# RMSNorm with GELU on one core: two rows a partition, gamma by matmul, VectorE in program order

## The chip, the cores and the metric

One core of one Trainium2 chip. The time is the device time of one execution in microseconds; the median of several runs is quoted. "Span" is the profiled execution, which is 1.8 us shorter than the time of the same run (333.7 against 335.53 before).

## The reference

```python
batch, seq_len, hidden = 8, 1024, 2048          # float32
rms = np.sqrt(np.mean(x ** 2, axis=-1, keepdims=True) + eps)
out = gamma * x / rms
return (0.5 * out * (1 + np.tanh(np.sqrt(2 / np.pi) * (out + 0.044715 * out ** 3)))).astype(np.float32)
```

There are 8192 rows of 2048 numbers. 67.1 MB are read and 67.1 MB written, and nothing is reused but gamma.

## The kernel before

A tile is 128 rows, one row a partition, 1 MB. Tiles are handled in groups of 4, then 2, then 1. Per tile: a load, a multiply by gamma on VectorE (into bf16), a square with a sum on ScalarE or VectorE (its elementwise result goes to PSUM, the accumulator memory, and is thrown away). Per group: eleven small VectorE steps that compute 1/rms. Then per tile a GELU on ScalarE, which writes over the tile's x buffer, and a store.

```python
    # group_sizes: 4 while more than 8 tiles are left, 2 while more than 4, then 1
    x_pool = ctx.enter_context(tc.tile_pool(name="xbuf", bufs=12))
    g_pool = ctx.enter_context(tc.tile_pool(name="gbuf", bufs=8))
    psum_pool = ctx.enter_context(tc.tile_pool(name="psum", bufs=2, space=bass.MemoryType.PSUM))

    gamma_sb = singles.tile([P, D], fp32)
    nc.sync.dma_start(out=gamma_sb, in_=gamma.partition_broadcast(P))
    # ... cut ...
    def emit_post(prev):
        tiles_p, xbufs_p, gbufs_p, inv_rms_p = prev
        for j, ti in enumerate(tiles_p):
            nc.scalar.activation(out=xbufs_p[j], in_=gbufs_p[j],
                func=mybir.ActivationFunctionType.Gelu_apprx_tanh, scale=inv_rms_p[:, j : j + 1])
            nc.scalar.dma_start(out=out_flat[ti * P : (ti + 1) * P, :], in_=xbufs_p[j])

    for ig, gsz in enumerate(group_sizes):
        # ... cut ...
        n_scalar_sq = gsz // 2
        for j, ti in enumerate(tiles):
            bx = x_pool.tile([P, D], fp32, name="bx")
            nc.sync.dma_start(out=bx, in_=x_flat[ti * P : (ti + 1) * P, :])
            bg = g_pool.tile([P, D], bf16, name="bg")
            nc.vector.tensor_tensor(out=bg, in0=bx, in1=gamma_sb, op=mybir.AluOpType.mult)
            scratch = psum_pool.tile([P, D], fp32, name="sq_scratch")
            if j < n_scalar_sq:
                nc.scalar.activation(out=scratch, in_=bx, ..., accum_out=ssq[:, j : j + 1])   # square
            else:
                nc.vector.tensor_tensor_reduce(out=scratch, in0=bx, in1=bx, ..., accum_out=ssq[:, j : j + 1])
        # ... cut: eleven steps of VectorE, ssq -> u -> yb -> w -> inv_rms, for the whole group ...
        if prev is not None:
            emit_post(prev)
        prev = (tiles, xbufs, gbufs, inv_rms)
    emit_post(prev)
```

The order of instructions in the text is not the order on the engines: the framework's scheduler sets that before the program is built, as the timeline in the prediction shows.

## Time and profile before

| | before |
|---|---|
| median of 4 runs | 335.43 us (335.31 to 335.54) |
| profile span | 333.7 us |
| VectorE, ScalarE busy | 249.0, 185.8 us |
| moved by the transfer engines | 135.32 MB in 18582 packets, mean 405 GB/s |
| VectorE waiting for loads of x | 67.1 us in 41 waits |

The page cuts the span into 40 equal slices and gives for each the busy tenths of every engine and the GB/s that the transfer engines moved. A packet is one piece of a transfer as the profile records it. The lines themselves are in the prediction below.

### The profile page before, as it was taken

To read this page: it belongs to the slowest core of one execution; us is meant where nothing else is said; L and a number is where in the kernel's file an instruction comes from. 1 tells how busy PE (TensorE), PEld (TensorE's weight loads), DVE (VectorE), ACT (ScalarE), POOL (GpSimd) and SP (SyncE) were. 2 spreads that over 40 slices of the span, in tenths; PEclk is the share of its full clock that TensorE was granted. 3 is DMA by queue.
4 is the path that set the end of the run, shared out by engine and by line. 5 is a ranking of instruction groups with operands and counts; after the bars stand their busy time and mean duration, and the time that the engine had idled before them with its cause. 6 is when DMAs were issued, how large, how long until landed. Compare 5 with 4: busy or idle time off the path is not lost.

```text
span 333.7 us, 850 instructions
## 1 busy us (share of the span) xinstructions
DVE 249.0 (75%) x353; ACT 185.8 (56%) x126; POOL 0.2 (0%) x4
## 2 busy tenths in 40 slices
DVE  0999998397785959768587876959777695956950
ACT  1442996748548274764728467373945824460391
POOL 0000000000000000000000000000000000000000
DMA  7999399999999999999999999999999999999298
GB/s 310 424 424 424 160 380 422 425 428 428 429 426 425 427 431 427 426 426 429 429 424 425 427 430 428 426 425 428 429 427 425 426 430 428 425 425 428 104 408 346
DMA packets 18582, 135.32 MB, mean 405 GB/s; under 512 B 2064, under 2 KB 2064, under 8 KB 2064
## 3 DMA queue, kind: packets, MB, share of 16 engines
q1 hardware_dynamic: 9360, 68.16, 48.4%
q10 hardware_dynamic: 9216, 67.11, 48.0%
q14 instruction: 6, 0.05, 0.0%
HBM read 68.16 MB, written 67.11 MB: 405 GB/s over the span
## 4 chain that ended last, share of the span: by engine, by line
DMA 80%; DVE 12%; ACT 4%; issue 1%; SPq 0%; ACTq 0%; DVEq 0%
DMA out_dram<-bx 74%; DMA bx<-in_x_dram 6%; DVE sq_scratch L107 6%; DVE bg L92 5%; ACT bx L62 4%; ACTq L68 0%; SPq L88 0%; DVE u L119 0%; DVE yb L133 0%; DVE w L141 0%; DVE w L140 0%; DVE yb L126 0%; DVE ssq L107 0%; DVE inv_rms L152 0%; DVE w L144 0%
## 5 line engine op out<-in xcount | busy, mean ns | idle before, releaser
L92 DVE TENSOR_TENSOR bg<-bx,gamma_sb 128x2048 bf16<-128x2048 f32 x64 | 146.3, 2290 | 67.2 <-DMA bx<-in_x_dram 67.1
L62 ACT ACTIVATE bx<-bg,inv_rms 128x2048 f32<-128x2048 bf16 x64 | 124.6, 1994 | 44.2 <-DVE inv_rms L169 23.1
L99 ACT ACTIVATE sq_scratch<-bx 128x2048 f32<-128x2048 f32 x30 | 56.2, 1874 | 96.2 <-DMA out_dram<-bx 50.9
L107 DVE CUSTOM_DVE_ANT_0 sq_scratch<-bx 128x2048 f32<-128x2048 f32 x34 | 77.4, 2307 | 0.0
L99 ACT ACTIVATION_READ_ACCUMULATOR sq_scratch<-bx 128x1 f32 x30 | 5.6, 186 | 0.0
L107 DVE DVE_READ_ACCUMULATOR2_ANT ssq<- 128x1 f32 x34 | 4.8, 142 | 0.0
L161 DVE TENSOR_SCALAR w<-w 128x4 f32<-128x4 f32 (+2 forms) x20 | 3.2, 166 | 0.5
L144 DVE TENSOR_SCALAR w<-w 128x4 f32<-128x4 f32 (+2 forms) x20 | 3.2, 166 | 0.4
L158 DVE TENSOR_TENSOR w<-w,u 128x4 f32<-128x4 f32 (+2 forms) x20 | 3.1, 161 | 0.5
L155 DVE TENSOR_TENSOR w<-inv_rms 128x4 f32<-128x4 f32 (+2 forms) x20 | 3.1, 160 | 0.5
L169 DVE TENSOR_TENSOR inv_rms<-inv_rms,w 128x4 f32<-128x4 f32 (+2 forms) x20 | 3.1, 160 | 0.5
L152 DVE TENSOR_TENSOR inv_rms<-yb,w 128x4 f32<-128x4 f32 (+2 forms) x20 | 3.1, 160 | 0.5
L141 DVE TENSOR_TENSOR w<-w,u 128x4 f32<-128x4 f32 (+2 forms) x20 | 3.1, 160 | 0.4
L133 DVE TENSOR_TENSOR yb<-magic_sb,yb 128x4 int32<-128x4 int32 (+2 forms) x20 | 3.1, 160 | 0.4
L140 DVE TENSOR_TENSOR w<-yb 128x4 f32<-128x4 f32 (+2 forms) x20 | 3.1, 160 | 0.4
L119 DVE TENSOR_SCALAR u<-ssq 128x4 f32<-128x4 f32 (+2 forms) x20 | 3.2, 162 | 0.2
L126 DVE TENSOR_SCALAR yb<-u 128x4 int32<-128x4 int32 (+2 forms) x20 | 3.1, 161 | 0.1
L99 ACT ACT_TABLE_LOAD x1 | 1.3, 1283 | 0.7 <-PEq L197 0.7
L62 ACT ACT_TABLE_LOAD x1 | 1.3, 1283 | 0.0
L57 DVE MEMSET magic_sb<- 128x4 int32 x1 | 0.1, 62 | 0.8 <-PEq L197 0.8
L197 POOL MEMSET const-bfloat16-1.0<- 128x1 bf16 x1 | 0.1, 101 | 0.0
L197 POOL MEMSET const-uint8-127<- 128x1 uint8 x1 | 0.1, 101 | 0.0
(2 smaller groups left out, 0.2 us busy)
## 6 DMA issues: line engine op xcount, KB each, us to landing
bx<-in_x_dram SPq DMA_DIRECT2D x64, 1024.0 KB, 10.4
out_dram<-bx ACTq DMA_DIRECT2D x64, 1024.0 KB, 19.5
gamma_sb<-in_gamma_dram SPq DMA_DIRECT2D x1, 1024.0 KB, 4.8
```

The source lines that it names most:

```text
L62: nc.scalar.activation(out=xbufs_p[j], in_=gbufs_p[j], func=mybir.ActivationFunctionType.Gelu_apprx_tanh, scale=inv_rms_p[:, j : j + 1],)
L92: nc.vector.tensor_tensor(out=bg, in0=bx, in1=gamma_sb, op=mybir.AluOpType.mult)
L99: nc.scalar.activation(out=scratch, in_=bx, func=mybir.ActivationFunctionType.Square, scale=inv_sqrt_d, accum_out=ssq[:, j : j + 1],)
L107: nc.vector.tensor_tensor_reduce(out=scratch, in0=bx, in1=bx, scale=1.0 / D, scalar=0.0, op0=mybir.AluOpType.mult, op1=mybir.AluOpType.add ...
L119: nc.vector.tensor_scalar(out=u[:, g], in0=ssq[:, g], scalar1=float(eps), scalar2=None, op0=mybir.AluOpType.add,)
L126: nc.vector.tensor_scalar(out=yb[:, g], in0=u[:, g].bitcast(i32), scalar1=1, scalar2=None, op0=mybir.AluOpType.logical_shift_right,)
L133: nc.vector.tensor_tensor(out=yb[:, g], in0=magic_sb[:, g], in1=yb[:, g], op=mybir.AluOpType.subtract,)
L140: nc.vector.tensor_tensor(out=w[:, g], in0=y0, in1=y0, op=mybir.AluOpType.mult)
L141: nc.vector.tensor_tensor(out=w[:, g], in0=w[:, g], in1=u[:, g], op=mybir.AluOpType.mult)
L144: nc.vector.tensor_scalar(out=w[:, g], in0=w[:, g], scalar1=-0.5, scalar2=1.5, op0=mybir.AluOpType.mult, op1=mybir.AluOpType.add,)
L152: nc.vector.tensor_tensor(out=inv_rms[:, g], in0=y0, in1=w[:, g], op=mybir.AluOpType.mult)
L161: nc.vector.tensor_scalar(out=w[:, g], in0=w[:, g], scalar1=-0.5, scalar2=1.5, op0=mybir.AluOpType.mult, op1=mybir.AluOpType.add,)
```

## The change

The intent: two consecutive rows a partition, so that a load or a store is 2 MB and each partition's piece is 16 KB in one run; 8 x buffers of 2 MB in place of 12 of 1 MB; groups of one chunk at the head and at the tail, of two in the middle; of each chunk, one row's square on ScalarE and the other's on VectorE; gamma read as one 8 KB row and spread to the partitions by a matmul with ones instead of a 1 MB broadcast; and VectorE's instructions kept in the order of the program. The core of the diff (cut: the same renaming in the loop, and the eleven steps, which don't change):

```diff
+R = 2
+NXBUF = 8
+NGBUF = 4
...
+        x_wide = x_flat.rearrange("(a r) d -> a (r d)", r=R)
+        out_wide = out_flat.rearrange("(a r) d -> a (r d)", r=R)
...
+        head = [1, 1]
+        tail = [1, 1, 1, 1]
+        mid_size = 2
...
-    x_pool = ctx.enter_context(tc.tile_pool(name="xbuf", bufs=12))
-    g_pool = ctx.enter_context(tc.tile_pool(name="gbuf", bufs=8))
+    x_pool = ctx.enter_context(tc.tile_pool(name="xbuf", bufs=NXBUF))
+    g_pool = ctx.enter_context(tc.tile_pool(name="gbuf", bufs=NGBUF))
...
-    nc.sync.dma_start(out=gamma_sb, in_=gamma.partition_broadcast(P))
+    gamma_row = singles.tile([1, D], fp32)
+    nc.scalar.dma_start(out=gamma_row, in_=gamma.rearrange("(o d) -> o d", o=1))
+    ones_row = singles.tile([1, P], fp32)
+    nc.vector.memset(ones_row, 1.0)
+    gamma_ps = psum_pool.tile([P, D], fp32, name="sq_scratch")
+    for k in range(D // 512):
+        nc.tensor.matmul(
+            gamma_ps[:, k * 512 : (k + 1) * 512],
+            lhsT=ones_row,
+            rhs=gamma_row[:, k * 512 : (k + 1) * 512],
+            start=True,
+            stop=True,
+        )
+    nc.vector.tensor_copy(out=gamma_sb, in_=gamma_ps)
...
-            if j < n_scalar_sq:
+                    on_scalar = r == 0
...
-        tile_rmsnorm_gelu_kernel(tc, *args)
+        with tc.manual_schedule(engines={_mybir.EngineType.DVE}):
+            tile_rmsnorm_gelu_kernel(tc, *args)
```

## The prediction

> **What bounds the kernel now.** I read the page first: the engines' shares, then the 40 slices, then the chain that ended last.
>
> ```profile
> DVE 249.0 (75%) x353; ACT 185.8 (56%) x126; POOL 0.2 (0%) x4
> DMA  7999399999999999999999999999999999999298
> GB/s 310 424 424 424 160 380 422 425 428 428 429 426 425 427 431 427 426 426 429 429 424 425 427 430 428 426 425 428 429 427 425 426 430 428 425 425 428 104 408 346
> DMA packets 18582, 135.32 MB, mean 405 GB/s; under 512 B 2064, under 2 KB 2064, under 8 KB 2064
> DMA 80%; DVE 12%; ACT 4%; issue 1%; SPq 0%; ACTq 0%; DVEq 0%
> ```
>
> No compute engine is full (VectorE 75%), but the transfers are at 9 tenths in 36 of the 40 slices, at one flat rate of about 427 GB/s. The chain is 80% transfers. So the kernel is bound by bytes over 427 GB/s, except in four slices that stand out: 0 (310), 4 (160), 37 (104) and 39 (346). I cut the span there with the table by stretches (columns: length, VectorE, ScalarE, GpSimd busy, granted clock, DMA share, GB/s).
>
> ```profile
> 2.00:34.00 32.00, 25.60 (x20) 10.96 (x12) 0.00 (x0) 1.00 1.01 421
> 34.00:39.00 5.00, 4.82 (x20) 4.68 (x5) 0.00 (x0) 1.00 0.08 33
> 39.00:57.00 18.00, 16.45 (x21) 13.84 (x8) 0.00 (x0) 1.00 0.98 388
> 57.00:311.00 254.00, 191.71 (x235) 143.41 (x98) 0.00 (x0) 1.00 1.01 427
> 311.00:317.00 6.00, 6.00 (x38) 2.47 (x2) 0.00 (x0) 1.00 0.03 11
> 317.00:333.00 16.00, 4.39 (x24) 9.21 (x5) 0.00 (x0) 1.00 0.95 393
> ```
>
> There are two holes. The reads of gamma and of the first 12 tiles (all the x buffers there are) end near 34 us; no store is in flight until 39, because ScalarE's first GELU starts at 36.67. Near the end, the stores that were queued run out at 311 and the next begins at 317. The timeline tells why in both places: VectorE isn't late for want of speed, its order is bad.
>
> ```profile
> 24.02 0.16 DVE L119 TENSOR_SCALAR u<-ssq 128x4 f32<-128x4 f32 x1
> 24.10 2.28 DVE L92 TENSOR_TENSOR bg<-bx,gamma_sb 128x2048 bf16<-128x2048 f32 x1
> 26.30 0.16 DVE L126 TENSOR_SCALAR yb<-u 128x4 int32<-128x4 int32 x1
> 26.37 2.29 DVE L92 TENSOR_TENSOR bg<-bx,gamma_sb 128x2048 bf16<-128x2048 f32 x1
> 28.57 0.15 DVE L133 TENSOR_TENSOR yb<-magic_sb,yb 128x4 int32<-128x4 int32 x1
> ...
> 314.53 3.89 ACT L62 ACTIVATE bx<-bg,inv_rms 128x2048 f32<-128x2048 bf16 x2 [14.68 <-DVE inv_rms L169]
> ```
>
> The first group's sum of squares is complete at 24.0, and its eleven small steps (0.2 us apart where nothing comes between) would end near 26.2. They are interleaved with the next group's 2.29 us passes and end at 36.6. At the end ScalarE waits 14.68 us for the same kind of result.
>
> **What the Trainium skill says.** "DMA: Bandwidth & Descriptors", section Specifications, gives a fabric ceiling of 435 GB/s for a core; the trace agrees, 427 in the middle. The same page, section "Issuing engines are not separate DMA queues", says that queues of different engines interleave on the same 16 engines; the trace agrees: the two queues hold 48.4% and 48.0%, and reads alone (421 from 2 to 34 us, its ramp included) are no faster than reads and writes together. "VectorE: DVE Perf Modes", section "Why PSUM operands drop a tier", says that a float32 operand in PSUM leaves VectorE at its basic rate; no copy from PSUM is in this trace, so I take the 2.29 us of a 128x2048 pass for it. So the big passes and the transfer rate are both near what they can be, and what is left to win is bytes and holes.
>
> **The change, part by part.**
>
> *Gamma.* The 1.05 MB broadcast goes; an 8 KB row takes its place. At 427 GB/s that takes 2.5 us off the transfers. Added: four matmuls and one VectorE copy. The first multiply began at 8.10. Now: row landed at about 3 us (a guess, from the 2.2 us after which the first bytes came before), some 4 to 6 us for four cold float32 matmuls (a guess, no matmul is in this trace), 2.3 for the copy: 9 to 11 us. A late start of up to 3 us, off the path unless it opens the first hole again.
>
> *VectorE in program order.* Per 2 MB chunk (two rows a partition): two multiplies and one square, 2.2 us apart each and 0.14 for the read, 6.8 us; then 2.2 us for the small steps per group. The first group is one chunk: 10.5 + 6.8 + 2.2 = 19.5 us, GELU twice 1.99, so the first store is issued near 24 us instead of 40.6 (the second row's end is what issues it).
>
> *More x buffers.* 8 x 2 MB instead of 12 x 1 MB. 16.8 MB at 427 GB/s keep reads alone going until 2.3 + 39 = 41 us; with stores from 25 us on they last longer. So hole one should close. Check for a second one: VectorE finishes chunk 1 at about 29, chunks 2 and 3 at 45, chunks 4 and 5 at 61. Just before the stores of 4 and 5 come (65 us), the transfers could have moved (65 - 2.3) x 427 GB/s = 26.8 MB, 12.8 chunks; there is work for 4 stores and 8 to 12 reads. Close, but covered, about 3 chunks (15 us) of margin.
>
> *The middle.* A pair of chunks is 8.4 MB both ways, 19.6 us at 427. VectorE needs 2 x 6.8 + 2.2 = 15.9 us of that, ScalarE 2 x 2.07 + 4 x 1.99 = 12.1. Transfers remain the bound. A buffer's turn may take 8 x 9.8 = 78 us; a load at half rate some 12, from landing to GELU 30 to 35, leaving 30 for the store. The four-deep bf16 buffers are two groups and are freed before VectorE returns to them.
>
> *The tail.* From the last landing: 6.8 + 2.2 on VectorE, 4.0 GELU, some 1.7 to get the store going: 14.7 us until the last chunk's store can move bytes. With 8 buffers, six or seven chunks are then unwritten; the others alone are 25 us or more of stores. Hole two should close.
>
> *Sum.* Lost now against 427 GB/s: 34-39 us 4.6; 39-57 1.6; 311-317 5.9; 317-333 1.3, of which 0.9 is only the drain at the end, so 0.4; gamma 2.5. Total 15.0 us, so 335.4 - 15.0 = 320.4. From the other side: 134.2 MB at 427 is 314.3; plus slice 0's deficit (8.34 x (1 - 310/427) = 2.3) and slice 39's (1.6), plus 1.8 between profile span (333.7) and profiled run's time (335.53): 320.0.
>
> *Longer rows.* 16 KB instead of 8 KB per packet, half as many packets. A packet of 8 KB takes on average some 307 ns at 427 GB/s (8192 x 16 / 427); at the skill's ceiling of 435 it would be 301. If the 6 ns are a cost per packet, half comes back, 1%: 3 us. No run here has shown that, so I take a third of it: 319.
>
> **The rivals.**
> *A. VectorE becomes the bound.* In strict order it can't fill a wait with other work, and it starts later. For: total work is about 247 us, and a new wait for GELU to free a bf16 buffer, or for ScalarE's square, stalls everything behind it. Against: 15.9 of 19.6 us per pair, and 67 us of today's idle time is waiting for loads. If it cost 0.5 us a pair more than the slack, little would show; if hole one came back in part, 322 to 327.
> *B. The tail comes out longer.* The last unit is 2 MB, so its own store alone is 4.9 us instead of 2.5, and its compute is twice as long. For: if too few stores are queued at the last landing, up to 10 us are exposed. Against: the count of buffers above. It would make 323 to 329.
> *C. Bigger rows change the transfer rate.* Better: up to 435 in the middle, 308.4 + 5.7 = 314. Worse: another pattern of addresses lowers it; 1% is 3 us.
> *D. The holes only move.* If the time were set by transfers alone and the holes refilled elsewhere, only gamma's 2.5 us would be won: 333, within 2%. Against: the middle is flat, with nothing to give back.
>
> **Range and chances.** 319 in the middle; low 315 (C better, all closed), high 325 (a hole of 5 or 6 us remaining under A or B). The 2% line is 328.7; it needs A or B in full, or D. Faster 0.93, within 2% 0.06, slower 0.01.
>
> **What would show it.** Slices 4 and 37 at 420 or more; the first store issued near 24 us; bytes 134.3 MB; packets of data halved; the middle between 425 and 432 GB/s; VectorE still about 247 us busy and mostly waiting for loads of x; the chain at 85% transfers or more. A slice under 350 between the first and the last would show A or B; a flat middle at another rate, C. I'm wrong altogether if VectorE shows waits for GELU or ScalarE of over 10 us in sum on the path, or if the middle falls under 420.

## The result

320.22 us (median of 8 runs, 320.13 to 320.45) against 335.47 us (12 runs on the same chips): a ratio of 0.9547, with a 95% interval of 0.9537 to 0.9556, so 4.5% faster. Ratios here and below are the mean time of one kernel's fast runs over that of the other's of the same rounds, so not quite the ratio of the medians quoted. The range was 315 to 325, the middle 319.

The same lines of the page after the change: the engines' shares, the slices, the packets, the chain.

```profile
PE 7.2 (2%) x8; PEld 2.5 (1%) x8; DVE 251.6 (79%) x340; ACT 188.1 (59%) x130; POOL 0.2 (0%) x4
...
DMA  7999999999999999999999999999999999999995
GB/s 293 430 432 393 432 428 425 434 430 430 428 431 434 434 434 428 428 434 427 430 428 428 438 436 432 428 428 430 432 430 428 428 431 434 436 429 430 428 434 237
DMA packets 9223, 134.27 MB, mean 422 GB/s; under 512 B 1025, under 2 KB 1025, under 8 KB 1025
...
DMA 58%; DVE 24%; issue 5%; ACT 4%; PE 2%; SPq 0%; DVEq 0%; ACTq 0%
```

Slices 4 and 37, which were 160 and 104 GB/s, are 432 and 428. Between the first and the last slice nothing is under 393. The flat part stands at about 431 instead of 427. What is worse is the last slice, 237 instead of 346. The table by stretches, cut where the holes were (columns: length, TensorE, its weight loads, VectorE, ScalarE, GpSimd busy, granted clock, DMA share, GB/s):

```profile
34.00:39.00 5.00, 0.00 (x0) 0.00 (x0) 5.00 (x4) 4.58 (x5) 0.00 (x0) 1.00 0.99 426
39.00:57.00 18.00, 0.00 (x0) 0.00 (x0) 17.55 (x21) 10.66 (x9) 0.00 (x0) 1.00 1.01 433
57.00:298.00 241.00, 0.00 (x0) 0.00 (x0) 206.45 (x283) 155.99 (x108) 0.00 (x0) 1.00 1.01 431
...
286.30:300.00 13.70, 0.00 (x0) 0.00 (x0) 8.57 (x15) 9.69 (x6) 0.00 (x0) 1.00 1.01 433
300.00:314.50 14.50, 0.00 (x0) 0.00 (x0) 0.00 (x0) 0.00 (x0) 0.00 (x0) 1.00 1.01 433
314.50:318.40 3.90, 0.00 (x0) 0.00 (x0) 0.00 (x0) 0.00 (x0) 0.00 (x0) 1.00 0.08 34
```

The 34 to 39 us stretch was at 33 GB/s and is at 426. The last load of x lands at 286.3; from there to 314.5 the stores alone keep the rate at 433, long after the last compute has ended. Then there is a drain of nearly 3 us that was under 1 us before: in the packet records of the last store, 13 of the 16 engines complete by 315.3, 15 by 315.8 and the last at 317.15. Before, all 16 completed between 332.4 and 332.6.

The start, from the timeline:

```profile
10.78 2.29 DVE L80 COPY gamma_sb<-sq_scratch 128x2048 f32<-128x2048 f32 x1 [9.80 <-PE sq_scratch L73]
...
22.13 1.28 ACT L92 ACT_TABLE_LOAD   x1 [6.58 <-DVE inv_rms L210]
23.43 3.90 ACT L92 ACTIVATE bx<-bg,inv_rms 128x2048 f32<-128x2048 bf16 x2
...
27.35 0.38 ACTq L98 DMA_DIRECT2D out_dram<-bx  x1
```

The eleven small steps of the first group now run without a big pass between them. The first store is issued at 27.35 us instead of 38.70 (and it holds two rows; before, the second row's store followed at 40.6), long before the 16.8 MB of loads in the eight buffers could run out. The waits, in sum over the span:

```profile
ACT sq_scratch L140 <- DMA bx<-in_x_dram: 83.4, 14, 7.8
DVE bg L126 <- DMA bx<-in_x_dram: 24.6, 15, 3.0
ACT bx L92 <- DVE inv_rms L210: 15.1, 5, 7.3
```

VectorE waits almost only for loads, as a kernel bound by its transfers should; 24.6 us in all.

The span can be put together from the slices: 134.2 MB at 431 GB/s are 311.4 us; slice 0 lost 7.96 x (1 - 293/431) = 2.5, slice 3 0.7, slice 39 3.6. The sum is 318.2, against 318.4 measured.

### The profile page after: what moved, and what is told of

It reads as the page before. It is cut to its first block, busy times and chain, and to the rows that moved or that the text cites.

```text
span 318.4 us, 704 instructions
## 1 busy us (share of the span) xinstructions
PE 7.2 (2%) x8; PEld 2.5 (1%) x8; DVE 251.6 (79%) x340; ACT 188.1 (59%) x130; POOL 0.2 (0%) x4
## 4 chain that ended last, share of the span: by engine, by line
DMA 58%; DVE 24%; issue 5%; ACT 4%; PE 2%; SPq 0%; DVEq 0%; ACTq 0%
DMA out_dram<-bx 38%; DMA bx<-in_x_dram 19%; DVE bg L126 13%; DVE sq_scratch L148 7%; ACT bx L92 4%; PE sq_scratch L73 2%; DMA gamma_row<-in_gamma_dram 1%; DVE w L185 0%; DVE yb L167 0%; DVE w L202 0%; DVE u L160 0%; DVE yb L174 0%; DVE w L182 0%; DVE inv_rms L193 0%; DVE w L196 0%
## 5 line engine op out<-in xcount | busy, mean ns | idle before, releaser
L126 DVE TENSOR_TENSOR bg<-bx,gamma_sb 128x2048 bf16<-128x2048 f32 x64 | 143.7, 2287 | 24.7 <-DMA bx<-in_x_dram 24.6
L140 ACT ACTIVATE sq_scratch<-bx 128x2048 f32<-128x2048 f32 x32 | 60.1, 1879 | 85.0 <-DMA bx<-in_x_dram 83.4
L148 DVE CUSTOM_DVE_ANT_0 sq_scratch<-bx 128x2048 f32<-128x2048 f32 x32 | 73.4, 2293 | 0.0
L73 PE MATMUL sq_scratch<-gamma_row,ones_row 1*128 1x512 f32 x8 | 7.2, 1072 | 3.6 <-DMA gamma_row<-in_gamma_dram 3.6
L160 DVE TENSOR_SCALAR u<-ssq 128x4 f32<-128x4 f32 (+1 forms) x19 | 3.2, 170 | 1.9
L202 DVE TENSOR_SCALAR w<-w 128x4 f32<-128x4 f32 (+1 forms) x19 | 3.2, 170 | 0.7
L185 DVE TENSOR_SCALAR w<-w 128x4 f32<-128x4 f32 (+1 forms) x19 | 3.2, 170 | 0.7
L167 DVE TENSOR_SCALAR yb<-u 128x4 int32<-128x4 int32 (+1 forms) x19 | 3.2, 170 | 0.6
L182 DVE TENSOR_TENSOR w<-w,u 128x4 f32<-128x4 f32 (+1 forms) x19 | 3.1, 162 | 0.7
L174 DVE TENSOR_TENSOR yb<-magic_sb,yb 128x4 int32<-128x4 int32 (+1 forms) x19 | 3.1, 162 | 0.7
L210 DVE TENSOR_TENSOR inv_rms<-inv_rms,w 128x4 f32<-128x4 f32 (+1 forms) x19 | 3.1, 162 | 0.7
L181 DVE TENSOR_TENSOR w<-yb 128x4 f32<-128x4 f32 (+1 forms) x19 | 3.1, 162 | 0.7
L199 DVE TENSOR_TENSOR w<-w,u 128x4 f32<-128x4 f32 (+1 forms) x19 | 3.1, 161 | 0.7
## 6 DMA issues: line engine op xcount, KB each, us to landing
bx<-in_x_dram SPq DMA_DIRECT2D x32, 2048.0 KB, 16.1
out_dram<-bx ACTq DMA_DIRECT2D x32, 2048.0 KB, 27.5
```

The costliest lines, as they stand in the source:

```text
L73: nc.tensor.matmul(gamma_ps[:, k * 512 : (k + 1) * 512], lhsT=ones_row, rhs=gamma_row[:, k * 512 : (k + 1) * 512], start=True, stop=True,)
L126: nc.vector.tensor_tensor(out=bg[:, s], in0=bx[:, s], in1=gamma_sb, op=mybir.AluOpType.mult)
L140: nc.scalar.activation(out=scratch, in_=bx[:, s], func=mybir.ActivationFunctionType.Square, scale=inv_sqrt_d, accum_out=scol,)
L148: nc.vector.tensor_tensor_reduce(out=scratch, in0=bx[:, s], in1=bx[:, s], scale=1.0 / D, scalar=0.0, op0=mybir.AluOpType.mult, op1=mybir.A ...
L160: nc.vector.tensor_scalar(out=u[:, g], in0=ssq[:, g], scalar1=float(eps), scalar2=None, op0=mybir.AluOpType.add,)
L167: nc.vector.tensor_scalar(out=yb[:, g], in0=u[:, g].bitcast(i32), scalar1=1, scalar2=None, op0=mybir.AluOpType.logical_shift_right,)
```

## The experiments

The theory of the prediction: the time is bytes over a flat rate, plus the stretches in which no transfer is queued; the change wins by closing two such holes, and 2.5 us by gamma's bytes. The rivals: the gains of the parts simply add whatever the holes do; the buffers rather than the order close the holes; the rate gained comes from something other than the longer packets. The runs undo one part of the change, or do one part alone. "Before" was timed beside them: 335.30 (beside the two parts alone, both together, and the change without the order), 335.52 (beside the change itself, the broadcast, one row, and separate packets), 335.57 us (beside the last four: pairs at the tail, six buffers, groups of two, four rows). Every kernel gave correct results.

### One part alone: gamma

```diff
 # the kernel before, with
-    nc.sync.dma_start(out=gamma_sb, in_=gamma.partition_broadcast(P))
+    # the 8 KB row, the four matmuls and the copy of the change
```

> The kernel before with only the gamma part of the change (8 KB row, matmul, copy), VectorE still in the scheduler's order. Theory of holes (time = bytes over 427 GB/s plus the stretches in which nothing is queued): the bytes saved lie before the first hole, whose end is set by the first GELU, so they win nothing; the compiled order puts the copy from PSUM (over at about 13 us in the trace after) and 13 big passes ahead of the first inv_rms, so the first GELU comes near 45 us instead of 36.7 and the first hole grows to some 15 us: 343 to 346 us, slower. Rival (the parts simply add, gamma is worth its 1.05 MB): 333 us.

Measured: 344.23 us (343.83 to 344.98), ratio 1.0267. Slower, as the theory of holes had it, and nowhere near the 333 of the sum of parts. The slices and the first GELU:

```profile
GB/s 309 428 420 313 0 145 384 417 424 424 420 428 425 427 428 428 427 427 428 428 427 425 428 427 425 426 427 428 427 428 426 426 426 426 426 428 427 143 382 352
```

```profile
45.63 3.89 ACT L75 ACTIVATE bx<-bg,inv_rms 128x2048 f32<-128x2048 bf16 x2 [4.69 <-DVE inv_rms L182]
```

The loads run out 2 us earlier (by the packets, 32.9 instead of 34.9) and the first GELU comes 9 us later. There are two reasons, of about equal size: VectorE's first pass after gamma starts 5.0 us later (13.12 instead of 8.10), and the scheduler, given another program, puts 14 passes of 2.2 us ahead of the first 1/rms where there were 12. Slice 4 is empty. The same edit that is worth 2.3 us inside the change (below) costs 8.9 us here.

### One part alone: VectorE's order

```diff
 # the kernel before, with
+        with tc.manual_schedule(engines={_mybir.EngineType.DVE}):
```

> The kernel before with only VectorE put in program order. Theory of holes: first inv_rms near 24 us, first store issued near 28 instead of 40.6, before the 12 loads have run out; the tail's waits go as well: both holes close, 335.4 - 12.5 = 323 us, no slice under 380 between the first and the last, middle still 427 GB/s. Rival (the order alone does not do it, the 12 MB of buffers or the groups of 4 leave a hole): 326 us or more with a slice under 300.

Measured: 328.13 us (328.06 to 328.27), ratio 0.9785. My 323 was wrong. The first hole closed; the second only moved.

```profile
GB/s 313 423 428 388 428 425 429 426 428 428 426 429 428 427 428 426 428 430 425 427 428 427 429 426 428 426 427 428 429 426 428 427 428 428 426 427 428 427 255 257
```

The cause stands in the timeline of the end:

```profile
312.56 2.00 ACT L62 ACTIVATE bx<-bg,inv_rms 128x2048 f32<-128x2048 bf16 x1 [4.58 <-DMA out_dram<-bx]
...
316.86 0.14 DVE L107 DVE_READ_ACCUMULATOR2_ANT ssq<- 128x1 f32 x1
...
319.14 2.00 ACT L62 ACTIVATE bx<-bg,inv_rms 128x2048 f32<-128x2048 bf16 x1 [4.57 <-DVE inv_rms L169]
```

The last four groups are single tiles. Each costs VectorE a multiply, a square (for a group of one, `gsz // 2` gives ScalarE none) and eleven steps: 6.58 us from one GELU to the next. A tile's store takes 2.45 us at 427 GB/s. So the queued stores run out, near 315, before the last GELU at 319. (The first of these waits is put down to a store, but VectorE's 1/rms ended just then too: the same 6.58 us.) It is no longer the order but VectorE's work per small group.

### The order, and pairs at the tail

```diff
 # the kernel before, program order, and
         if left > 8:
             g = 4
-        elif left > 4:
-            g = 2
         else:
-            g = 1
+            g = 2
```

> The kernel before in program order on VectorE, and its last four groups of one tile made two groups of two, so that the eleven small steps run once per two tiles and ScalarE takes one square of each pair. Theory: what kept program order alone at 328 is VectorE in the last groups (6.58 us per single tile against 2.45 us of store); per pair it is 9.0 us, so the tail closes: 322.5 to 324 us, no slice under 380 before the last. Rival (the 12 MB of buffers leave too few stores queued): 326 us or more, slice 38 still low.

Measured: 325.03 us (324.69 to 325.14), ratio 0.9686.

```profile
GB/s 324 420 429 371 427 427 429 426 430 426 425 430 428 425 431 426 429 428 426 428 427 426 429 427 425 430 425 430 427 427 430 426 427 428 427 425 430 427 428 246
```

The tail is full until the last slice: two lines of Python fewer in the group sizes are worth 3.1 us on top of the order, with 12 buffers of 1 MB as before. So neither the 16 MB of buffers nor the wide chunks are what closes the holes. It is 1 us above my range all the same, and slice 3, where the first stores begin, is at 371, below the 380 that I had named. Now that both holes are closed the last slice is 246, as in the change: the drain at the end.

### The order and gamma together

```diff
 # the kernel before, with both edits: gamma by matmul, and
+        with tc.manual_schedule(engines={_mybir.EngineType.DVE}):
```

> The kernel before with the gamma part and the program order, but with its 1 MB tiles, 8 KB rows, groups and 12 buffers. Theory of holes: with no hole left the 2.5 us of gamma's bytes now count: 320 to 321.5 us, middle 427 GB/s; then the wider chunks and the bigger buffers of the change are worth about nothing. Rival (the late gamma, 13 us, leaves the first hole in part open with 12 MB of buffers): 323 to 326 us, a slice under 350 near 35 us.

Measured: 326.99 us (326.44 to 327.18), ratio 0.9747.

```profile
GB/s 301 426 422 422 390 404 413 425 428 425 428 426 428 426 428 425 429 426 428 425 426 430 424 430 425 427 426 429 426 429 425 429 425 428 426 428 426 427 239 258
```

Neither number held, because the hole of the tail was still there (slices 38 and 39 at 239 and 258). Against the order alone gamma is worth 1.1 us here, not 2.5. Slices 4 to 6 are at 390, 404 and 413: against 427 that is 8.13 x (0.087 + 0.054 + 0.033) = 1.4 us lost. But the order alone lost 0.7 us itself, in slice 3 (388). So the later start of VectorE accounts for some 0.7 us of the missing 1.4; slice 38 (239 against 255) for 0.3 more and slice 0 (301 against 313) for 0.2. The rival had the right place and the wrong size: it asked for a slice under 350.

### The change without the order

```diff
-        with tc.manual_schedule(engines={_mybir.EngineType.DVE}):
-            tile_rmsnorm_gelu_kernel(tc, *args)
+        tile_rmsnorm_gelu_kernel(tc, *args)
```

> The changed kernel without the program order on VectorE. Theory of holes: the compiled order puts 12 big passes between the copy of gamma and the first inv_rms, so the first store is issued near 45 us and its bytes move near 46.5, while the 16.8 MB of loads end at 41: a first hole of about 5 us, 325 us; the tail stays closed as six or seven chunks are unwritten at the last landing. Rival (buffers of 16 MB alone are enough to bridge both holes): 320 to 321 us. Rival (the order matters at both ends): 330 us.

Measured: 324.49 us (324.38 to 324.67), ratio 0.9676.

```profile
GB/s 294 439 427 431 427 229 390 388 425 423 441 437 422 427 441 433 423 435 438 427 423 437 435 429 427 437 433 427 429 439 431 425 436 435 425 428 435 437 423 272
```

One hole, in slice 5, where the loads of eight buffers end; the first GELU is at 40.65 us. The tail is closed. So in the changed kernel the order is worth 4.2 us at the head and nothing at the tail, which is full without it too. That the stores still queued cover a bad order there is the theory's reading; no run isolated it.

### The change with the broadcast of gamma

```diff
-    # 8 KB row, matmuls, copy
+    nc.sync.dma_start(out=gamma_sb, in_=gamma.partition_broadcast(P))
```

> The changed kernel with gamma read by the 1 MB broadcast again. If gamma is worth its bytes once no hole is left: 320.2 + 1.05 MB / 431 GB/s = 322.6 us. Rival (it was only worth something through VectorE's start): VectorE starts about 3.5 us earlier and nothing is lost, 320 us or less.

Measured: 322.61 us (322.46 to 322.69), beside 320.31 (320.19 to 320.45) of the change itself on the same chip, whose expectation was:

> The changed kernel again, on the same chip as the next three, to compare with: 320.2 us, middle 431 GB/s, last slice low (engines finish up to 2.5 us apart), packets of the first microseconds slow.

The difference, 2.3 us, is the 1.05 MB at 431 GB/s (2.4). VectorE started earlier and the first store was issued 4 us earlier:

```profile
23.44 0.38 ACTq L85 DMA_DIRECT2D out_dram<-bx  x1
```

None of that helped: with no hole left, the start of the compute is off the path, and bytes are on it.

### One row a partition, and two rows in separate packets

First the change with its switch at one row (1 MB transfers, 8 KB packets, the same bytes of buffers):

```diff
-R = 2
-NXBUF = 8
-NGBUF = 4
+R = 1
+NXBUF = 16
+NGBUF = 8
```

> The changed kernel with its switch at one row: 1 MB tiles, 8 KB packets, 16 x and 8 bf16 buffers, so the same bytes of buffers. If the cost is per packet or per transfer the middle falls from 431 to 427 GB/s, 2.8 us more of transfer; if the slow first packets and the late engine at the end belong to 16 KB packets, up to 3 us come back: 320 to 323 us in all. If the rate came from something else (program order, buffers), the middle stays 431.

Then the 2 MB transfers, but with a partition's two rows 128 rows apart in memory, so that each packet is 8 KB:

```diff
-        x_wide = x_flat.rearrange("(a r) d -> a (r d)", r=R)
+        x_wide = x_flat.rearrange("(c r p) d -> c p r d", r=R, p=P)
 # and the same for out_wide
```

> The changed kernel with the same 2 MB transfers, but each partition's two rows are 128 rows apart in memory, so a transfer has 256 packets of 8 KB instead of 128 of 16 KB. Cost per packet: middle 427 GB/s, like one row a tile. Cost per transfer (completion, issue): middle stays 431. Slow first packets, if they belong to 16 KB packets: gone, last slice fuller.

Measured, beside 320.31: 324.71 us (324.38 to 324.99) with one row, 322.60 (322.35 to 322.73) with two rows in separate packets. The middle of each, in the table by stretches: first the change, then two rows in separate packets, then one row.

```profile
60.00:280.00 220.00, 0.00 (x0) 0.00 (x0) 190.12 (x252) 142.50 (x98) 0.00 (x0) 1.00 1.01 431
```

```profile
60.00:280.00 220.00, 0.00 (x0) 0.00 (x0) 186.37 (x245) 139.33 (x95) 0.00 (x0) 1.00 1.01 428
```

```profile
60.00:280.00 220.00, 0.00 (x0) 0.00 (x0) 174.81 (x220) 127.04 (x89) 0.00 (x0) 1.00 1.01 427
```

The cost is per packet: with the same order, buffers and sizes of transfer, 8 KB packets move 428 and 16 KB packets 431 GB/s. At these rates (427.7 and 431.0, counted from the packet records of the same stretch) 134.2 MB differ by 2.4 us, against 2.3 measured. Transfers of 2 MB instead of 1 MB are worth hardly more than rounding, 427.2 to 427.7. The edit also changes which addresses a packet covers, and no run separates that from its length; but the packet times at three lengths, below, fit a fixed cost. The slow first packets, and the drain at the end, are there with 8 KB packets too (last slices 230 and 175), so they don't belong to the packet size: that rival is out.

The one-row kernel is slower by 2.1 us more than its packets explain. At its end each single tile has its own eleven steps on VectorE, and two GELUs wait 2.25 and 4.52 us for 1/rms; from 316 to 318 us the transfers are at 20 GB/s. It is a smaller form of the tail seen above. In two rows a partition, one series of eleven steps serves two rows.

### Six x buffers

```diff
-NXBUF = 8
+NXBUF = 6
```

> The changed kernel with 6 x buffers (12.6 MB, as before) instead of 8. If the added 4 MB carry part of the gain: the first loads end at 31 us, and just before the stores of chunks 2 and 3 (53 us) about 10 chunks of transfer are available against 10.3 that could have moved, so small holes near 50 and 65 us: 322 to 324 us. Rival (buffers only matter in the scheduler's order): 320 to 321 us.

Measured: 327.74 us, unusually scattered (325.70 to 330.55), ratio 0.9774: faster than before, but unclear whether by 2%. The profiled run took 329.64, near the slow end of the scatter. Worse than expected, and not only at the head, which is where I had looked:

```profile
60.00:280.00 220.00, 0.00 (x0) 0.00 (x0) 172.22 (x218) 126.37 (x87) 0.00 (x0) 1.00 1.00 411
```

The middle falls to 411 GB/s, with slices down to 328. A buffer's turn is six chunks of 9.8 us, 59 us. The prediction's own count of a turn (load 12, from landing to GELU 30 to 35, then the store) leaves 12 to 17 us for the store, and a store that shares the rate needs about as much. The 12.6 MB that were enough as twelve 1 MB tiles (order and pairs) are too few as six 2 MB chunks. That the number of chunks is the reason is this count's reading, as the two kernels differ in more; the run with four rows, at the same bytes as the change, points the same way. Beside it on the same chip the next kernel, which does not differ from the change in time, took 320.24, so the two buffers are worth 7.5 us, give or take the 2 us of its scatter.

### Groups of two throughout

```diff
-        head = [1, 1]
-        tail = [1, 1, 1, 1]
+        head = [2]
+        tail = [2]
```

> The changed kernel with all 16 groups of two chunks, no single-chunk groups at head and tail. By the count of queued work the first store would be issued near 34 us, still before the 16.8 MB of loads end at 41, and the last store could start about 19 us after the last landing, within the 25 us of stores then unwritten: no hole, 320 to 321 us. Rival (small groups at the ends are needed): 323 us or more, with a slice under 350.

Measured: 320.24 us (320.06 to 320.35), ratio 0.9545: the same as the change. With eight buffers the small groups at the ends are worth nothing.

### Four rows a partition

```diff
-R = 2
-NXBUF = 8
-NGBUF = 4
+R = 4
+NXBUF = 4
+NGBUF = 2
...
-        mid_size = 2
+        mid_size = 1
...
-                    on_scalar = r == 0
+                    on_scalar = r % 2 == 0
```

> The changed kernel with four rows a partition: 32 KB packets, 4 MB transfers, 4 x buffers and 2 bf16 buffers of the same bytes in sum, groups of one chunk. If the cost is a fixed 5.6 ns per packet (8 KB: 307.0 ns at 427 GB/s, 16 KB: 608.4 at 431), the middle is 433 GB/s where it is full, 1.4 us of transfer less. But only four buffers turn, and the last chunk's work is twice as long: if that opens holes, 322 to 330 us; if not, 319 us.

Measured: 333.20 us (332.17 to 335.31), ratio 0.9936. The rate is there while loads alone run, in the stretch before the first store, but four buffers can't hold it:

```profile
3.00:33.00 30.00, 7.11 (x8) 2.42 (x8) 21.87 (x24) 11.62 (x10) 0.00 (x0) 1.00 1.00 433
48.00:56.00 8.00, 0.00 (x0) 0.00 (x0) 8.00 (x6) 7.97 (x7) 0.00 (x0) 1.00 0.74 283
```

433 GB/s is what the fixed cost per packet gave, but that is weak evidence: packets of 32 KB are coarse, and stretches around this one give 426 to 439. The durations are the better measure. The median packets are 0.309, 0.611 and 1.213 us for 8, 16 and 32 KB: doubling 0.309 gives 0.618 and doubling 0.611 gives 1.222, so 7 to 9 ns are paid per packet by the durations. By the rates it is less, 2 x 306.5 - 608.2 = 5 ns for 8 against 16 KB (each packet's bytes over a sixteenth of 427.7 and 431.0 GB/s). The holes cost far more: 333.2, even over the 330 that I had given as the worst.

No version beat the change: groups of two tie with it, all others are slower.

## Why the prediction was right

**The two holes.** Right. Their stretches went from 33 and 11 GB/s to 426 (34 to 39 us) and 433 (300 to 314.5 us), and the runs show each hole with its cause: the first comes back without the order (slice 5 at 229); the second stays in the kernel before with single tiles at the tail (255 and 257), goes with pairs, and shows again, smaller, in the change with one row. One sentence of it was too simple. "VectorE isn't late for want of speed, its order is bad" holds for the first hole; for the second, order alone left VectorE with 6.58 us per single tile, a want of speed in that stretch. Two readings of the start were off without consequence: the first group's sums are complete at 22.0, not 24.0 (the steps were already waiting behind a multiply; in order they end at 24.1, not 26.2), and 40.6 is the time of the second store, the first being issued at 38.70.

**Gamma.** 2.5 us of bytes: 2.3 measured in the changed kernel. It is bound to the condition that the first hole is closed; alone it cost 8.9 us. The late start was mis-sized: 9 to 11 us guessed, the copy ended at 13.0, because the matmuls took 7.2 us, not 4 to 6. The Trainium skill would have given it: "FP8 and Floating Point Precision" counts four passes for true float32, and "TensorE: Matmul & The Clock Gate", section "Back-to-back issue gap", gives N / 1.2 ns a matmul while the array is cold; 4 matmuls x 4 passes x 427 ns is an estimate of 6.8 us, and the trace has 7.16 (in eight records, 0.85 us from one weight load to the next). The copy from PSUM took 2.29 us, as the prediction had assumed; the multiply and the square are at 2.29 too, and no run tried to make these passes faster. I also left out the load of ScalarE's table, 1.28 us. So the first store came at 27.35, not 24. It made no difference. The margin was counted at 15 us, which takes the upper end of its "4 stores and 8 to 12 reads"; the lower end, 12 chunks against 12.8, would have left a small hole, and none came.

**The head's margin, the middle and the tail.** Right. VectorE and ScalarE fit in the middle, and the last chunk's store was issued at 299.34, 13 us after the last landing at 286.3 (14.7 was counted until its first bytes). From the last landing the transfers still moved (300 - 286.3) x 433 + 14.5 x 433 GB/s = 12.2 MB before the drain, about six chunks, as counted. The count of a buffer's turn, 78 us with little to spare, is borne out by the run with six. In the change a load takes 16.1 us from issue to landing (12 guessed) and a store 27.5 (30 left for it), in the median.

**Longer rows.** A cost per packet is shown by the run with separate packets and the packet times at three lengths; the size is 2.3 us, and I had taken 1 of 3.

**The sum.** Without the longer rows the prediction was 320.0 to 320.4; the run with 8 KB packets took 322.6. So holes and gamma gave back 12.9 us (335.5 - 322.6), not 15.0. The missing 2 us lie mostly in the last slice, whose deficit I had carried over from before as 1.6 us: it was 3.6. The 1.3 us of packets that I had not counted on made up for most of it. The hit within 1.2 us owes something to this cancellation.

**Rival A** (VectorE as the bound) and **B** (a longer tail) didn't occur, though each shows up in a neighbour: A in single tiles at the tail, and a shortage of buffers with six. **C** was right in its milder form. **D**, that only gamma's bytes would be won, is refuted by the order alone (328.1).

**A check that failed.** "The chain at 85% transfers or more": it is 58%, with VectorE at 24%. The chain is followed back from the last instruction, and from 13 to 95 us it runs through VectorE, which was catching up on its late start and had no wait in that stretch. The slices show the transfers full all the while. The chain's share is no measure of what bounds a kernel whose queue is kept full: it names one chain of releases, and the queued work beside it hides how much of it could have been late.

**What stays open.** Why one engine ends up to 2 us after the others once no hole is left. That holes go with it is shown: in the six runs with a hole near the end, the 16 engines' last packets end within 0.15 to 0.19 us; in the six with none at all they are 2.6 to 3.0 us apart, and in the two whose holes lie earlier (the change without the order, six buffers) 1.8 and 1.1. So a hole lets late engines catch up, and part of what closing it gave back is lost in the drain. What makes an engine late is not shown. In the records, the program's own instruction fetches (five 8 KB packets in the changed run after the start) each come within 0.4 us of a single slow packet, and the excess of these five, 2.2 us in sum, is about the size of the lateness; but the kernel before has such fetches too, and which engine a packet ran on isn't recorded, so this is a suspicion. Nor is it shown why packets of x run at up to 2.8 times their usual time in the first microsecond or so, and up to 2.3 times for 2 us around the first stores (0.7 to 0.8 us of transfer each time).

## What to carry to other kernels

When the row of transfer rates is flat but for a few slices, count what each slice lost and ask what was queued there; a part of a change is worth its bytes only where no hole swallows them, and the same part can cost time where it moves the end of a hole. Check program order on the engine that releases the first and the last stores, and its work per group in the tail, before touching the flat part. Count buffers in turns (chunks times the time of a chunk), not only in bytes: doubling the chunk to 4 MB at the same bytes undid nearly all of the gain here (333.2 us).

## What the Trainium skill lacked or had wrong

- "DMA: Bandwidth & Descriptors", section "Rules for kernel authors", asks for 128 partitions and at least 1 MiB per transfer for the most bandwidth. Beyond that, the length of the packet counts, not the size of the transfer: 427.2 GB/s with 1 MB transfers of 8 KB packets, 427.7 with 2 MB of 8 KB, 431.0 with 2 MB of 16 KB, that is about 5 ns per packet (7 to 9 by the packets' durations).
- The same page, section "Why small descriptors are slow (HBM only)", works out its fixed cost per packet for a descriptor of 256 bytes alone. Here going from 8 KB to 16 KB was still worth 2.3 us of 322.6.
- The same page, section "Latency and other measured facts", says that two of the 16 engines are usually slower. No page says how far the engines of one long stream drift apart, or that a hole brings them together: here the last engine ended at 317.15 us when 13 of 16 had ended by 315.3; in the kernel before, with a hole shortly before the end, all ended within 0.2 us.
